# Tokens in a row for the state-space input product, and distant queries and keys stored by remainder

## The chip, the cores and the metric

The kernel runs on one core of one Trainium2 chip. The metric is device microseconds of one execution. A profiled execution of the kernel before gives the trace; its clock of TensorE (PE) was granted at 0.987 of full speed as a mean over the span.

## The reference, cut to what matters

Two blocks run one after the other on 1024 tokens of width 1024. The first has a gated MLP branch, a state-space (S5) branch and a mixture of experts; the second has dilated attention and a recurrent branch. All weights and activations are f32. Two places matter here.

```python
h = rms_norm(x, norm1_g[l])
p = h @ w_in[l]
uv = jax.nn.gelu(p[..., :o_s5], approximate=False)
s_in = p[..., o_s5:o_gate]          # 256 columns, the state-space input
...
DILATION_GROUPS = ((128, 1), (512, 4), (2048, 16))
...
# query t attends to t, t-r, t-2r, ..., t-window
t = t.astype(jnp.float32).reshape(B, L, dilation, H, Dh).transpose(0, 2, 1, 3, 4)
...
s = jnp.einsum('brnqhd,brnkhd->brnhqk', qs, kb) * (Dh ** -0.5)
```

There are three attention groups of four heads with 128 columns each. With 1024 tokens the second group works on four remainders of 256 tokens, and the kernel handles the third by eight remainders of 128 tokens and a mask for every other one.

## The kernel before, in words

**Big products.** Every f32 factor of a big product is split into a high and a low part (`K.split`: ScalarE copies the high part, L219; VectorE subtracts, L220), and `K.mm3` issues three matmuls per product, all recorded at L225. Attention's small products and the transposes (L228) use f32 directly; one such product is two matmul instructions, one transpose is one. Instructions of an engine run in the order in which they were laid out at compile time; a list scheduler of the framework lays them out by readiness, so an order can differ from the text of the program.

**State-space input.** `block1` loads the transposed x in eight pieces of 128 channels (`raw`, split into `xh`, `xl` by L1106 and L1107) and makes the product with the 256 state-space columns of `w_in` first. Its stationary operand takes every eighth token: `sl = slice(j, T, 8)`, so that for each of eight j the 128 rows of the result are tokens j, j+8, and so on. Eight pieces times eight j times three are 192 matmuls of 256 columns into four PSUM banks `ps_s`. ScalarE then copies them to `ss` with the token's norm as scale (L1166). The norms come from x read a second time by rows (`xj`, L1146, in tiles `m0` to `m3` twice over), squared on ScalarE (L1147), a reciprocal root on VectorE (`rsqrt`), and for the other layouts a diagonal `rd` (L1151), a product with ones on PE (L225, `ps<-m,sm`), `r_bc` (L1156) and `r_t` (L1158, L1159). `project(512, 0, ...)`, the first half of v, follows on PE with 192 matmuls of the same shape, whose stationary operands are 128 tokens in a row; its results fill the four other PSUM banks and wait there for `r_t` (gelu, L1174). The second half of v is next. `ss` is first read by the transposes of the first quarter of `s5` (L228, `ps<-sm,s`).

**Attention.** In `block2` the class `Pair` makes two output pieces of 128 columns by 1024 tokens with Strassen's seven half products, and hands halves to an output class by `one` (a ScalarE copy from PSUM, L389) or `two` (a VectorE sum of SBUF and PSUM, L394). `Spill` puts each 128x512 half into `st` (two buffers) and stores it in DRAM by SyncE (L390, L395). The first of a pair gets one `one` and one `two`, the second two `two`. The first twelve pairs of q, k and v hold group 0 beside group 1 of the same head (`near`); six pairs hold group 2. Beside later pairs, `Head` loads q, k and v of a head (L667, L671, L672) and works tile by tile: `scores` (L691 to L701), `turn` (transposes), `values`. In `scores` queries and keys are picked by `tok(g, m)`, 128 tokens in steps of 1, 4 or 8. A tile of width 256 has two products a block, one for the previous block of keys and one for the current one. `turn_v` transposes the values, picked by the same steps. `tick` advances this work by one step after each half product of a pair, so PE alternates between 12 matmuls of a pair and a step of attention.

```python
sl = slice(j, T, 8)
...
k.mm(pv[:, x, :128], s.q[:, tok(g, m)], s.kt[:, tok(g, m - back[g])], True, True)
k.mm(pv[:, x, W - 128:], s.q[:, tok(g, m)], s.kt[:, tok(g, m)], True, True)
```

Of the kernel before, what the change touches and what calls it, by code (L numbers as in the profile page):

```python
# [8 lines left out]
F32 = mybir.dt.float32  # L9
# [3 lines left out]
AF = mybir.ActivationFunctionType  # L13
# [7 lines left out]
T = 1024  # L21
# [133 lines left out]
class K:  # L155
    def __init__(s, tc, ins, ctx):
        s.tc, s.nc, s.i, s.ctx = tc, tc.nc, ins, ctx
        s.pp = ctx.enter_context(tc.tile_pool(name="pp", bufs=8, space=PSUM))
        s.dp = ctx.enter_context(tc.tile_pool(name="dp", bufs=1, space=DRAM))
        s.base = ctx.enter_context(tc.tile_pool(name="base", bufs=1))  # L160
        s.pool = s.base
        s.n = 0
        s.spare = {}
        s.last = {}
        s.turn = False
        s.wait = None
# [131 lines left out]
def bc(ap, axis, n):  # L298

    return ap.unsqueeze(axis).to_broadcast(list(ap.shape[:axis]) + [n] + list(ap.shape[axis:]))  # L300
# [57 lines left out]
def block2(k, out, dbg=None):  # L358
    nc, i, c = k.nc, k.i, k.c
    V, S, SY, GP = nc.vector, nc.scalar, nc.sync, nc.gpsimd  # L360
    dbg = dbg or {}
    ident = c("ident")
    MUL, ADD, SUB = OP.mult, OP.add, OP.subtract
    halves = [slice(0, 512), slice(512, 1024)]
# [4 lines left out]
    sq = k.t([128, SQW], "sq", pool=k.base)  # L369
# [11 lines left out]


    class Spill:
        def __init__(s, dst):
            s.dst = dst

        def one(s, h, p):
            st = k.t([128, 512], "st", 2)
            S.activation(st, p, AF.Copy)  # L389
            SY.dma_start(s.dst[:, halves[h]], st)  # L390

        def two(s, h, a, b):
            st = k.t([128, 512], "st", 2)
            V.tensor_tensor(st, a, b, op=ADD)  # L394
            SY.dma_start(s.dst[:, halves[h]], st)  # L395

    class Keep:
        def __init__(s, dst):
# [32 lines left out]
    qkv = {(n, g, j): dram(f"{n}d{g}{j}") for n in "qkv" for g in range(3) for j in range(4)}  # L431
    col = dict(q=Q0, k=K0, v=V0)
# [11 lines left out]

    w = lambda c: i["w_in2"][c // 128, 0]
    two = lambda c0, mk, x: tuple((w(c0 + y * 128), lambda y=y: mk(y)) for y in (x, x + 1))
    at = lambda n, g, j: (w(col[n] + g * 512 + j * 128), lambda: Spill(qkv[n, g, j]))
    near = [(at(n, 0, j), at(n, 1, j)) for j in range(4) for n in "qkv"]
    cols = []
    for f in range(0, 8, 2):  # L450
        cols += near[f:f + 2] + [two(U0, ukeep, f), two(GL0, lambda x: Spill(sgd[x]), f)]
    cols += near[8:]
    cols += [(at(n, 2, j), at(n, 2, j + 1)) for n in "qkv" for j in (0, 2)]
    cols += [two(GA0, lambda x: Spill(gad[x]), x) for x in (0, 2)]
    cols += [two(MG0, lambda x: Spill(mgd[x]), x) for x in (8, 10, 12, 14, 0, 2, 4, 6)]
    NI = len(cols)

# [198 lines left out]
    back = [1, 4, None]  # L656
    od = {(g, j): dram(f"od{g}{j}", (T, 130)) for g in range(3) for j in range(4)}
    otd = [dram(f"otd{j}") for j in range(4)]
    tok = lambda g, m: slice(toks[g][m][0], toks[g][m][0] + 127 * toks[g][m][1] + 1, toks[g][m][1])

    class Head:
# [20 lines left out]
        def scores(s, u):  # L682
            ms, W = tiles[s.g][u]
            g, n = s.g, len(ms)
            if u == 0:
                s.ss = k.t([128, 8, 2], "ss", 2)
            p = k.ps("pb")
            pv = p[:, :n * W].rearrange("p (m w) -> p m w", m=n)
            for x, m in enumerate(ms):
                if W == 256:  # L690
                    k.mm(pv[:, x, :128], s.q[:, tok(g, m)], s.kt[:, tok(g, m - back[g])], True, True)  # L691
                k.mm(pv[:, x, W - 128:], s.q[:, tok(g, m)], s.kt[:, tok(g, m)], True, True)
            s.sb = k.m(4)
            sv = s.sb[:, :n * W].rearrange("p (m w) -> p m w", m=n)
            mask = sq[:, SQ["mprev"][0]:SQ["mprev"][0] + 256] if W == 256 else cq("mtwo" if g == 2 else "mcur")
            V.tensor_tensor(sv, pv, bc(mask, 1, n), op=ADD)
            nm = s.ss[:, ms[0]:ms[0] + n, 1:2]
            V.tensor_reduce(nm, sv, axis=AX.X, op=OP.max, negate=True)
            V.tensor_scalar(nm, nm, SCALE, None, op0=MUL)
            for x, m in enumerate(ms):  # L700
                S.activation(sv[:, x, :], sv[:, x, :], AF.Exp, scale=SCALE, bias=s.ss[:, m, 1:2], accum_out=s.ss[:, m, 0:1])  # L701
# [121 lines left out]
    y, yh, yl, oh = (k.g("S", 12, dt) for dt in (F32, FR, FR, FR))  # L823
# [18 lines left out]
    def split(n, kk, src):  # L842
        h, l = part(n, kk)
        S.activation(h, src, AF.Copy)
        return V.tensor_tensor(l, src, h, op=SUB)  # L845
# [8 lines left out]
    def squares(half, t4, v):  # L854
        z = (a2 if half else F)[t4][:, :1024]
        return z, S.activation(z, xs[4 * half + t4], AF.Square, accum_out=v[:, t4:t4 + 1])
# [22 lines left out]
    for t4 in range(4):  # L879
        for h, hs in enumerate(halves):  # L880
            p = k.ps()
# [3 lines left out]
        z, sqd = squares(0, t4, va)  # L885
# [12 lines left out]
    for kk in range(8):  # L898
        dst = (a11 + a12)[kk]
# [35 lines left out]
    for kk in range(4):  # L935
        x = split("s4", kk, a12[kk])
# [102 lines left out]
    for m in range(8):  # L1039
        ga, y = k.m(m % 4), k.m(4 + m % 2)  # L1040
# [16 lines left out]
    for tt in range(8):  # L1057
# [4 lines left out]
        q = k.t([128, 2], "oq", 2)  # L1062
        fs, fb = [], k.g("gb")
        for h, hs in enumerate(halves):
            p = k.ps(("pa", "pb")[h])
# [9 lines left out]
        r = k.rsqrt(v, 1, "or")  # L1075
# [7 lines left out]
def block1(k, dbg=None):  # L1083
    nc, i = k.nc, k.i
    V, S, PE, SY, GP = nc.vector, nc.scalar, nc.tensor, nc.sync, nc.gpsimd
# [3 lines left out]
    c = lambda n: sm[:, SM[n][0]:SM[n][0] + SM[n][1]]  # L1089
# [9 lines left out]
    w_in, xT = i["w_in"], i["xT"]  # L1099
    ws_p, xh, xl = [], [], []  # L1100
    for kk in range(8):
# [3 lines left out]
        h, l = k.a(), k.a()  # L1105
# [7 lines left out]
    pv = [k.split(k.wload(w_in[2, q])) for q in range(2)]  # L1113


    ps_s = [k.ps("pb") for _ in range(4)]
    for kk in range(8):
        wh, wl = ws_p[kk // 4]
        for j in range(8):
            o = ps_s[j // 2][:, (j % 2) * 256:(j % 2) * 256 + 256]  # L1120
            sl = slice(j, T, 8)
            cs = slice((kk % 4) * 256, (kk % 4) * 256 + 256)
            k.mm3(o, xh[kk][:, sl], xl[kk][:, sl], wh[:, cs], wl[:, cs], kk == 0 and j % 2 == 0, kk == 7)

    vs = [k.g("U", 4, pool=k.pb) for _ in range(4)]

    def project(c0, hc, pc=None, pair=False):

        pc = pc or [k.split(k.wload(w_in[c0 // 256 + hc, q])) for q in range(2)]
        for tt in range(8):  # L1130
            if not pair or tt % 2 == 0:
                p = k.ps()
            o = p[:, tt % 2 * 256:tt % 2 * 256 + 256] if pair else p[:, :256]
            for kk in range(8):
                wh, wl = pc[kk // 4]
                cs = slice((kk % 4) * 256, (kk % 4) * 256 + 256)
                sl = slice(tt * 128, tt * 128 + 128)
                k.mm3(o, xh[kk][:, sl], xl[kk][:, sl], wh[:, cs], wl[:, cs], kk == 0, kk == 7)
            yield o, tt, vs[tt // 2][:, (tt % 2) * 512 + hc * 256:(tt % 2) * 512 + hc * 256 + 256]
# [13 lines left out]
    for h in range(2):  # L1153
        p = k.ps("pb")
# [4 lines left out]
    V.tensor_reduce(r_t, rd.rearrange("p (n t) -> p n t", n=8), axis=AX.X, op=OP.add)  # L1159


    ss = [k.g("s", 2) for _ in range(2)]
    for j in range(8):
        for hf in range(2):
            p = ps_s[j // 2][:, (j % 2) * 256 + hf * 128:(j % 2) * 256 + hf * 128 + 128].rearrange("p (g h) -> p g h", h=16)
            S.activation(ss[hf].rearrange("p (g j h) -> p g j h", g=8, j=8)[:, :, j, :], p, AF.Copy, scale=r_p[:, j:j + 1])  # L1166
    v0 = list(project(512, 0, pv, True))
    pv = [k.split(k.wload(w_in[3, q])) for q in range(2)]
    if "s" in dbg:
        for hf in range(2):  # L1170
            SY.dma_start(dbg["s"][:, hf * 1024:(hf + 1) * 1024], ss[hf])
# [55 lines left out]
    for q, n in enumerate(("lng", "lnb")):  # L1227
        a = i[n]
# [38 lines left out]
    for hf in range(2):  # L1267
        h, l = k.split(yT[hf], k.m(2 * hf, 1024, FR), k.m(2 * hf + 1, 1024, FR))
# [8 lines left out]
    for m in range(2):  # L1277
        sg = k.m(4 + m)
        for nh in range(2):
            p = k.ps()  # L1280
# [8 lines left out]
        h, l = k.split(sg, *((k.g("bb", 2, FR), k.g("bb", 2, FR)) if m == 0 else (k.g("r_bc", 1, FR, k.pb), k.g("yT", 2, FR, k.pb))))  # L1289
# [3 lines left out]
    for m in range(4):  # L1293
        h, l = k.g("ab", 8, FR), k.g("ab", 8, FR)
        for nh in range(2):
            p = k.ps("pb")
# [11 lines left out]
    for m in range(8):  # L1308
# [21 lines left out]
        for q in range(4):  # L1330
            h, l = (z.rearrange("p (m j c) -> p m j c", m=4, j=2)[:, m % 4] for z in mt[q][m // 4])
# [10 lines left out]
    for j in range(8):  # L1342
        xj = k.wload(xpv[:, j, :])
        for h in range(2):
            p = k.ps()
            hs = slice(h * 512, h * 512 + 512)
            for kk in range(8):
                sl = slice((kk % 4) * 256 + (j % 2) * 128, (kk % 4) * 256 + (j % 2) * 128 + 128)
# [596 lines left out]
def program(tc, ins, out):  # L1945
    with ExitStack() as ctx:
        k = K(tc, ins, ctx)
        block1(k)
        moe(k)
        block2(k, out)  # L1950
# [16 lines left out]
```

## Time and profile before

| what | us |
|---|---|
| runs: median of 3 (lowest to highest) | 2911.59 (2910.22 to 2913.25) |
| profiled execution, its own time | 2912.2 |
| span of its trace | 2910.4 |
| PE busy | 2804.7 |
| VectorE (DVE) busy | 2223.8 |
| ScalarE (ACT) busy | 1616.9 |

The span runs from the first to the last instruction; 1.8 us of the execution lie around it. In the trace PE is the matmul, PEld the load of the stationary operand that goes ahead of it, SPq the queue of SyncE that issues the DMAs. A tensor name such as `ps<-wh,A` is output, then the moving and the stationary operand. Matmuls overlap in the pipeline: the length of one is about 0.28 us or more, while the distance of their starts is what a stream costs.

### The profile page before, as it was taken

The numbers are of one execution on the slowest core, as the hardware profiler recorded it, in microseconds if no ns is written. First come the engines' busy times: TensorE is split into PE (matmuls) and PEld (weight loads), VectorE is DVE, ScalarE is ACT, GpSimd is POOL, SyncE is SP. The second block draws the span as 40 slices with busy tenths as digits, with TensorE's granted clock in tenths as the row PEclk, the third lists the DMA queues.
The fourth block names the chain that finished last, engine by engine and source line by source line (L and its number), as shares of the span: only waits on it lengthen the run. The fifth ranks groups of instructions, "written<-read, shape, count | busy, mean of one in ns | idle before, by whom it ended". The sixth has DMA issues, their size and how long they took to land. (4 is left out here: it accounts for less than half of the span.)

```text
span 2910.4 us, 37326 instructions
## 1 busy us (share of the span) xinstructions
PE 2804.7 (96%) x13441; PEld 2298.5 (79%) x13441; DVE 2223.8 (76%) x3619; ACT 1616.9 (56%) x2201; POOL 138.6 (5%) x106
## 2 busy tenths in 40 slices
PE   8999999949999999999999997999999999999998
PEld 8889887738888877777777775788888888888777
DVE  5967468589999888888888888878888554558774
ACT  4334334228888777777777776556665344444441
POOL 0000000020000000000000002100001100000000
PEclk9999999979999999999999999999999999999999
DMA  6123465558999999999999995223334644456762
GB/s 210 59 70 99 133 199 175 195 195 313 380 377 377 352 363 364 361 363 364 364 363 365 363 367 185 68 103 120 110 120 170 215 139 148 149 193 239 255 225 80
DMA packets 165993, 676.09 MB, mean 232 GB/s; under 512 B 18480, under 2 KB 28848, under 8 KB 125104
## 3 DMA queue, kind: packets, MB, share of 16 engines
q1 hardware_dynamic: 160912, 654.70, 61.5%
q0 software_dynamic: 4896, 19.01, 2.5%
q8 instruction: 105, 1.72, 0.2%
q14 instruction: 80, 0.66, 0.1%
HBM read 586.97 MB, written 84.57 MB: 231 GB/s over the span
## 5 line engine op out<-in xcount | busy, mean ns | idle before, releaser
L225 PE MATMUL ps<-A,wh 128*128 128x512 f32 x1920 | 603.5, 395 | 4.7 <-DVE A L845 1.9
L225 PEld LDWEIGHTS ps<-A,wh 128*128 128x128 f32 x1920 | 357.6, 188 | 81.1 <-DVE A L845 2.3
L225 PE MATMUL ps<-A,wl 128*128 128x512 f32 x960 | 375.6, 391 | 0.0
L1825 DVE TENSOR_TENSOR wl<-A,wh 128x1024 fp32r<-128x1024 f32 x253 | 308.8, 1221 | 38.7 <-ACT wh L1821 37.0
L1825 DVE TENSOR_TENSOR ml<-A,mh 128x1024 fp32r<-128x1024 f32 x253 | 308.5, 1219 | 9.2 <-ACT mh L1821 2.6
L225 PE MATMUL ps<-S,wh 128*128 128x512 f32 x960 | 306.1, 400 | 7.0 <-DVE u L530 4.8
L219 ACT ACTIVATE wh<-wr 128x512 fp32r<-128x512 f32 (+2 forms) x168 | 154.7, 922 | 242.9 <-PE ps L225 189.2
L1821 ACT ACTIVATE wh<-A 128x1024 fp32r<-128x1024 f32 x256 | 270.3, 1056 | 23.8 <-PE ps L225 23.8
L1821 ACT ACTIVATE mh<-A 128x1024 fp32r<-128x1024 f32 x256 | 270.2, 1055 | 20.9 <-PE ps L225 20.9
L220 DVE TENSOR_TENSOR wl<-wr,wh 128x1024 fp32r<-128x1024 f32 (+2 forms) x166 | 175.6, 1058 | 66.5 <-ACT wh L219 51.8
L225 PE MATMUL ps<-wl,xh 128*128 128x512 f32 x520 | 209.1, 402 | 10.1 <-DVE wl L1825 10.1
L225 PEld LDWEIGHTS ps<-S,wh 128*128 128x128 f32 x960 | 180.4, 191 | 47.4 <-DVE u L530 6.6
L225 PEld LDWEIGHTS ps<-A,wl 128*128 128x128 f32 x960 | 180.2, 188 | 39.5 <-issue 0.7
L225 PE MATMUL ps<-wh,xl 128*128 128x512 f32 x520 | 205.4, 395 | 0.0
L225 PE MATMUL ps<-ml,xh 128*128 128x512 f32 x520 | 204.1, 392 | 0.5 <-DVE ml L1825 0.5
L225 PE MATMUL ps<-mh,xl 128*128 128x512 f32 x520 | 203.2, 391 | 0.0
L225 PE MATMUL ps<-S,wl 128*128 128x512 f32 x480 | 190.5, 397 | 0.0
L225 PE MATMUL ps<-wh,xh 128*128 128x512 f32 x520 | 188.2, 397 | 0.0
L225 PE MATMUL ps<-mh,xh 128*128 128x512 f32 x520 | 186.7, 393 | 0.2 <-ACT mh L1821 0.2
L225 PE MATMUL ps<-wh,A 128*128 128x256 f32 (+1 forms) x704 | 159.5, 319 | 8.1 <-ACT wh L219 8.1
L225 PEld LDWEIGHTS ps<-wh,A 128*128 128x128 f32 x704 | 128.8, 218 | 12.4 <-ACT wh L219 8.1
L228 PE MATMUL ps<-sm,m 128*128 128x128 f32 (+1 forms) x692 | 102.2, 278 | 28.5 <-DVE m L1460 14.2
(508 smaller groups left out, 5534.2 us busy)
## 6 DMA issues: line engine op xcount, KB each, us to landing
A<-in_w_up_dram SPq DMA_DIRECT2D x125, 1024.0 KB, 8.0
A<-in_w_down_dram SPq DMA_DIRECT2D x65, 1024.0 KB, 7.1
A<-in_w_gate_dram SPq DMA_DIRECT2D x64, 1024.0 KB, 6.4
wr<-in_w_gate_dram SPq DMA_DIRECT2D x124, 512.0 KB, 7.1
mr<-in_w_down_dram SPq DMA_DIRECT2D x59, 1024.0 KB, 7.0
wr<-in_w_in_dram SPq DMA_DIRECT2D x82, 512.0 KB, 4.0
wr<-in_w_mod_dram SPq DMA_DIRECT2D x24, 512.0 KB, 4.4
wr<-in_w_ing_dram SPq DMA_DIRECT2D x16, 512.0 KB, 4.5
```

The costliest lines, as they stand in the source:

```text
L219: s.parts = (s.nc.scalar.activation(hi, raw, AF.Copy), (eng or s.nc.vector).tensor_tensor(lo, raw, hi, op=OP.subtract))
L220: (eng or s.nc.vector).tensor_tensor(lo, raw, hi, op=OP.subtract))
L225: s._pe(out, s.nc.tensor.matmul(out, a, b, start=start, stop=stop, skip_group_check=True))
L228: s._pe(out, s.nc.tensor.transpose(out, a, ident))
L1821: a = S.activation(h, raw, AF.Copy)
L1825: (GP if n < 6 else V).tensor_tensor(l, raw, h, op=OP.subtract)
```

## The change

The state-space product takes 128 tokens in a row as stationary operand. Its four banks are copied to SBUF (in the first half of each of the tiles `vs`, which are written for good only later), stored to a new DRAM tensor `sd` with one row per token, and read back with eight consecutive tokens per partition into `m0` and `m1`. The copies to `ss` then read these. The first half of v and the next weights stand ahead of the copies in the text.

`Spill` gets a step: 4 for queries and keys of group 1, 8 for those of group 2. The copy or sum reads both its inputs by remainder and writes `st` in runs of one remainder. For step 8 the store puts eight runs of 64 tokens (256 bytes) per partition into the rows of 128 tokens per remainder. `scores` then takes 128 neighbouring columns, and a tile of width 256 makes one product of 256 keys a block, in two runs of 128. Values stay in token order.

```diff
-        def __init__(s, dst):
-            s.dst = dst
+        def __init__(s, dst, step=1):
+            s.dst, s.step = dst, step
+
+        def of(s, *z):
+            st = k.t([128, 512], "st", 2)
+            if s.step == 1:
+                return st, (st,) + z
+            by = lambda y: y.rearrange("p (i r) -> p r i", r=s.step)
+            return st, (st.rearrange("p (r i) -> p r i", r=s.step),) + tuple(map(by, z))
 
         def one(s, h, p):
-            st = k.t([128, 512], "st", 2)
-            S.activation(st, p, AF.Copy)
-            SY.dma_start(s.dst[:, halves[h]], st)
+            st, (o, p) = s.of(p)
+            S.activation(o, p, AF.Copy)
+            s.put(h, st)
 
         def two(s, h, a, b):
-            st = k.t([128, 512], "st", 2)
-            V.tensor_tensor(st, a, b, op=ADD)
-            SY.dma_start(s.dst[:, halves[h]], st)
+            st, (o, a, b) = s.of(a, b)
+            V.tensor_tensor(o, a, b, op=ADD)
+            s.put(h, st)
+
+        def put(s, h, st):
+            if s.step == 8:
+
+                d = s.dst.rearrange("p (r h i) -> p h r i", r=8, h=2)
+                SY.dma_start(d[:, h], st.rearrange("p (r i) -> p r i", r=8))
+            else:
+                SY.dma_start(s.dst[:, halves[h]], st)
...
-    at = lambda n, g, j: (w(col[n] + g * 512 + j * 128), lambda: Spill(qkv[n, g, j]))
+    at = lambda n, g, j: (w(col[n] + g * 512 + j * 128), lambda: Spill(qkv[n, g, j], (1, 4, 8)[g] if n in "qk" else 1))
...
+                own = lambda z: z[:, m * 128:(m + 1) * 128]
+                keys = own(s.kt)
                 if W == 256:
-                    k.mm(pv[:, x, :128], s.q[:, tok(g, m)], s.kt[:, tok(g, m - back[g])], True, True)
-                k.mm(pv[:, x, W - 128:], s.q[:, tok(g, m)], s.kt[:, tok(g, m)], True, True)
+                    keys = s.kt.rearrange("p (m c) -> p m c", c=128)[:, m - back[g]:m + 1:back[g]]
+                k.mm(pv[:, x], own(s.q), keys, True, True)
...
-            sl = slice(j, T, 8)
+            sl = slice(j * 128, j * 128 + 128)
...
     vs = [k.g("U", 4, pool=k.pb) for _ in range(4)]
+    sd = k.dp.tile([T, 256], F32, name="sd", tag="sd")
+    for q, p in enumerate(ps_s):
+        z = vs[q][:, :512]
+        S.activation(z, p, AF.Copy)
+        SY.dma_start(sd[q * 256:(q + 1) * 256].rearrange("(n t) d -> t n d", t=128), z.rearrange("t (n d) -> t n d", n=2))
...
+    sq = [k.m(q) for q in range(2)]
+    for q in range(2):
+        SY.dma_start(sq[q], sd.rearrange("(c j) d -> c (j d)", j=8)[:, q * 1024:(q + 1) * 1024])
+    v0 = list(project(512, 0, pv, True))
+    pv = [k.split(k.wload(w_in[3, q])) for q in range(2)]
+
     ss = [k.g("s", 2) for _ in range(2)]
     for j in range(8):
         for hf in range(2):
-            p = ps_s[j // 2][:, (j % 2) * 256 + hf * 128:(j % 2) * 256 + hf * 128 + 128].rearrange("p (g h) -> p g h", h=16)
+            p = sq[j // 4][:, (j % 4) * 256 + hf * 128:(j % 4) * 256 + hf * 128 + 128].rearrange("p (g h) -> p g h", h=16)
             S.activation(ss[hf].rearrange("p (g j h) -> p g j h", g=8, j=8)[:, :, j, :], p, AF.Copy, scale=r_p[:, j:j + 1])
-    v0 = list(project(512, 0, pv, True))
-    pv = [k.split(k.wload(w_in[3, q])) for q in range(2)]
```

## Rows read from the trace of the kernel before

**Rows 1.** The page, part 1: busy time and share of each engine.

```profile
PE 2804.7 (96%) x13441; PEld 2298.5 (79%) x13441; DVE 2223.8 (76%) x3619; ACT 1616.9 (56%) x2201; POOL 138.6 (5%) x106
```

**Rows 2.** Busy time by stretch (first line: the columns).

```profile
core 0: us, PE busy (x) PEld busy (x) DVE busy (x) ACT busy (x) POOL busy (x), PEclk, DMA share, GB/s
12.00:54.90 42.90, 42.90 (x181) 42.90 (x180) 21.04 (x104) 18.62 (x26) 2.12 (x2) 1.00 0.76 266
55.20:66.40 11.20, 11.20 (x96) 11.20 (x95) 4.42 (x17) 3.75 (x11) 0.49 (x1) 1.00 0.22 70
...
1860.00:2280.00 420.00, 413.60 (x1777) 336.27 (x1778) 330.35 (x420) 222.46 (x259) 24.74 (x23) 0.99 0.39 134
2280.00:2600.00 320.00, 318.82 (x1695) 277.87 (x1694) 165.95 (x275) 142.50 (x361) 0.00 (x0) 1.00 0.46 153
```

**Rows 3.** PE in order of time: start, length, line, [idle before <-releaser].

```profile
54.87 0.52 PE L225 MATMUL ps<-wh,A 128*128 128x256 f32 x2
...
66.49 1.88 PE L225 MATMUL ps<-m,sm 128*128 128x512 f32 x4
```

**Rows 4.** VectorE in order of time, block1.

```profile
23.91 1.28 DVE L1107 SCALAR_TENSOR_TENSOR A<-wr,sm,A 128x1024 fp32r<-128x1024 f32 x1 [0.59 <-ACT A L1106]
...
59.53 1.22 DVE L1151 TENSOR_TENSOR m<-sm,rqy 128x1024 f32<-128x1024 f32 x1
...
70.30 1.22 DVE L1159 TENSOR_REDUCE r_t<-m 128x8 f32<-128x1024 f32 x1
```

**Rows 5.** ScalarE in order of time, block1.

```profile
32.27 1.06 ACT L219 ACTIVATE wh<-wr 128x1024 fp32r<-128x1024 f32 x1 [5.93 <-PE ps L225]
33.23 1.04 ACT L1147 ACTIVATE m<-m 128x1024 f32<-128x1024 f32 x1
...
43.43 1.06 ACT L1147 ACTIVATE m<-m 128x1024 f32<-128x1024 f32 x1
...
55.31 1.06 ACT L219 ACTIVATE wh<-wr 128x1024 fp32r<-128x1024 f32 x1 [10.73 <-PE ps L225]
59.45 2.69 ACT L1166 ACTIVATE s<-ps,rqy 128x128 f32<-128x128 f32 x10 [3.08 <-DVE rqy L272]
```

**Rows 6.** SyncE's queue: x read by rows (L1146), its issues and their landing.

```profile
22.53 15.31 SPq L1146 DMA_DIRECT2D m<-in_xp_dram  x8
...
DMA to landing us min/median/max: 3.6/5.6/9.0
```

**Rows 7.** PE in order of time: the first reader of `ss`.

```profile
107.65 0.66 PE L228 MATMUL ps<-sm,s 128*128 128x128 f32 x4
```

**Rows 8.** PE in order of time: score products (L225) and a transpose of values (L228).

```profile
2301.42 1.06 PE L225 MATMUL ps<-m,m 128*128 128x128 f32 x8
2309.12 0.61 PE L225 MATMUL ps<-m,m 128*128 128x128 f32 x4
2316.22 2.12 PE L225 MATMUL ps<-m,m 128*128 128x128 f32 x8
...
2321.39 1.12 PE L228 MATMUL ps<-sm,m 128*128 128x128 f32 x8
...
2545.58 2.18 PE L225 MATMUL ps<-m,m 128*128 128x128 f32 x8
```

**Rows 9.** PE in order of time: f32 products of 256 columns in `s5`.

```profile
140.07 1.03 PE L225 MATMUL ps<-m,s5E 128*128 128x256 f32 x4
...
141.38 0.60 PE L225 MATMUL ps<-m,s5E 128*128 128x256 f32 x2
```

**Rows 10.** Groups by line and shape: xcount, busy us, mean ns, idle before.

```profile
L394 DVE TENSOR_TENSOR st<-u,ps 128x512 f32<-128x512 f32 x96 | 65.4, 681 | 61.3 <-PE ps L225 59.7 <-DMA vd<-st 1.3
...
L220 DVE TENSOR_TENSOR A<-m,A 128x256 fp32r<-128x256 f32 x32 | 19.8, 669 | 0.4
...
L1179 DVE TENSOR_TENSOR U<-U,gt 128x256 f32<-128x256 f32 x16 | 6.6, 419 | 9.8 <-ACT gt L1178 9.8
```

**Rows 11.** DMA issues with median landing time (2250 to 2700 us), and one pair's stores.

```profile
qd<-st SPq DMA_DIRECT2D x8, 256.0 KB, 2.3
...
2298.25 8.43 SPq L395 DMA_DIRECT2D qd<-st  x3
```

## The prediction

> **What bounds the kernel now.** I read the page first: PE is busy for 2804.7 us of the span, the next engine for 2223.8 [rows 1]. A share is a mean, so I took both stretches that the change touches. While the state-space input runs (12 to 54.9 us) and while attention runs beside the projections (2280 to 2600 us) PE has next to no gap, 42.9 of 42.9 and 318.8 of 320, at a full clock, with VectorE at about half [rows 2]. So a microsecond less of PE's stream should be a microsecond less of the whole, unless a wait appears that PE's own slowness hid. Then I compared paces of matmuls that differ in nothing but the step between their stationary columns; that is where the gain must come from. Last came the chains that PE's slowness hides: the norms [rows 3 to 6] and the way of the halves out of PSUM [rows 10, 11].
>
> **State-space product.** Before, 181 matmuls start in 42.9 us, 0.237 us each; right behind them the first half of v, with the same shape, moving weights and x tiles but 128 tokens in a row, starts 96 in 11.2 us, 0.117 each [rows 2]. The pace changes where the operand changes, at 55 us [rows 3]. 192 x 0.120 = **23.1 us** less. Can x come fast enough? The last low part of x is ready at 25.2 us [rows 4]; a piece then needs 24 x 0.117 = 2.8 us, eight 22.4, so PE, starting near 8 and held a little by the first weights, ends at about 32 and not at 55. Bound below: if x held it all the same, the end is still no later than 25.2 + 2.8 plus the pieces behind it, so little is lost.
>
> **What is late next.** PE's queue holds, 11.3 us behind the end of the product, the product of ones with `rd` (66.49 us) [rows 3]; everything behind it on PE waits for it. `rd` needs all eight squares. Before, the first square started at 33.23 because ScalarE stood 5.93 us before it, waiting for PE to free a weight buffer [rows 5]; that wait goes, as the fourth piece ends near 21. x by rows is issued from 22.53 and lands after 5.6 us [rows 6], so I put the first square at 29 and the last, as before 10.2 us behind it [rows 5], to end near 40. From the end of the last square (44.5) to the end of `rd` (60.75) went 16.3 us [rows 4, 5], of which some 10 are the weight split behind ScalarE's 10.73 us wait for PE's end of product [rows 5]; 6 remain. So `rd` is ready near 46. PE arrives at 32 + 11.3 = 43.4 if the ones keep their place, and near 38 if they move up, since their bank now comes free by four early copies and not by the copies to `ss`. The stall is 2 to 8 us: I take **5**, the middle, and keep 0 and 8. `r_t` came 5.0 us behind the ones [rows 3, 4], so near 52, while the first half of v then ends near 61: no second stall.
>
> **The way through DRAM.** Added: four copies of 128x512 on ScalarE (a copy of 1024 columns takes 1.06 us [rows 5]; half of that and a fixed part, so about 0.6 each), four stores, two loads. It ends near 50 and `ss` some 6 us later; the first reader on PE stood at 107.65 [rows 7], so near 90 after the change. The cover is 30 us; without it the whole trip, about 15 us, would be paid. The stores go on SyncE's queue, and what waits behind a waiting store there is the loads of x by rows: that is a rival. The 16 copies to `ss` stay; they read SBUF. Cost: 0.
>
> **Scores.** Eight instructions take 1.06 us with steps of 1, 2.12 with steps of 4 (group 1) and 2.18 with steps of 8 (group 2) [rows 8]. Group 1 has three such tiles per head, group 2 two, four heads each: 12 x 1.06 + 8 x 1.12 = **21.7 us** less. The products of 256 keys give nothing more: an f32 instruction of 256 columns costs (1.03 - 0.60) / 2 = 0.215 us [rows 9], two of 128 columns 2 x (1.06 - 0.61) / 4 = 0.225 [rows 8], so 88 pairs give 0.9 at most. I take 22 for both. Nothing waits longer for scores: the turn that follows stands behind the same 12 matmuls as before.
>
> **The halves on their way out.** The steps do not vanish, they move to VectorE and ScalarE. 28 sums (8 pairs of group 1 with two, 4 of group 2 with three) and 4 copies now read by remainder. No row has a strided operand in PSUM. The nearest is the split of 128x256 with one operand in steps of 8: 0.669 us against 0.419 for a plain sum of that size [rows 10], 0.25 more per 256 columns, so 0.50 more on 0.681 for a sum. Below, nothing; above, both operands pay, 1.0. I take 0.5, since that row is the same engine and step: 14 us of VectorE. VectorE stands idle 61.3 us ahead of 96 such sums, nearly all waiting for PE [rows 10], and PE lost only 6.4 of 420 us in the busiest part, VectorE at 79% [rows 2]. I charge **1.5 us**, with 0 and 6 as ends.
>
> [...]
>
> **DMA.** 16 stores of group 2 write runs of 256 bytes in place of 2 KB. They land in 2.3 us now; three stores of a pair take 8.43 us, about 4 apart, and the two buffers leave roughly 7 us before a third sum needs the first again [rows 11]. So up to threefold landing costs nothing, and attention reads group 2 last. Cost: 0.
>
> **Sum.** 23.1 - 5 + 22 - 1.5 = 38.6 us less. The profiled execution took 2912.2 us (span 2910.4 and 1.8 around it); that gives 2873.6, and the median of the runs shown is 0.6 below it: **2873 us**.
>
> **Rivals.**
> *No stall* (0.24): the ones stand later on PE or the squares end sooner. For it: x lands as early as 3.6 us [rows 6]. Against it: the bank comes free earlier. 5 us better: 2868.
> *The queue* (0.14): the stores of `sd` stand on SyncE ahead of x by rows, as in the text. Then x starts near 36, when the copies are done, in place of 22.53; the last square, 22 us behind the first issue before with 4.6 of them the weight buffer's wait [rows 5, 6], ends near 53, `rd` near 59, and PE stalls 17 us, not 5: 2885. Against it: before, what was ready first was queued first.
> *The step is not the cause* (0.04): the values' transposes take their stationary operand in steps of 4 and need only 1.12 us for eight [rows 8]. If the state-space product is slow by something else, 18 us go: 2891. Against it: the same tiles at half the cost right behind it.
> *The stores* (0.04): if runs of 256 bytes land after 10 us, 12 sums wait 2.6 us each, up to 31: 2904. [...]
> *Slower: the sums hold PE* (0.04). A sum frees PE's bank, and the splits of the next pair queue behind it. Its cover is 61.3 / 96 = 0.64 us [rows 10]. To eat 40 us, 28 sums must each exceed this by 1.45, so from about 2.8 us a sum the kernel is slower; at 3.2 it ends near 2924. Against it: that is eight times the extra that the split's row shows.
>
> **Numbers.** My forecast has 0.50. Faster by over 0.2% (5.8 us, about what a measurement of this kernel can tell from no change) are all but the last rival and a sliver between: 0.95, same 0.01, slower 0.04. The range takes in the forecast with its ends (stall 0 to 8, sums 0 to 6), *no stall* and *the queue*: 2862 to 2889.
>
> **What would show it.** PE at about 0.117 us per matmul from 8 us, the first half of v starting near 32, a wait of PE for `rd` near 43, copies to `ss` done before 60, PE's first reader of `ss` some 18 us earlier. In attention 1.06 for every full score tile. `st` sums near 1.2 us and no new wait of PE for them. Wrong if the product keeps 0.24, if SyncE's stores precede x by rows, or if PE waits for `st` or `u` by tens of microseconds.

## The result and the profile after

Four runs of the changed kernel have a median of 2874.03 us (2868.33 to 2875.23); four of the kernel before, on the same chip, 2911.38 (2910.22 to 2913.25). The ratio, estimated from all of these runs, is 0.9868, 95% interval 0.9853 to 0.9882: faster, by 37 us, 1 us from the forecast. The profiled execution took 2875.23 us, its span 2873.5, the mean granted clock 0.987 in both kernels.

First the page, part 1, of the changed kernel, beside [rows 1].

```profile
PE 2763.0 (96%) x13353; PEld 2253.5 (78%) x13353; DVE 2232.4 (78%) x3619; ACT 1618.4 (56%) x2205; POOL 138.4 (5%) x106
```

PE is busy 41.7 us less and the span is 36.9 us shorter; VectorE gained 8.6 us of work, so it stands idle 45.5 us less. The bound is the same. Then the stretches [rows 2]: the start, the state-space product, and the two of attention, which come some 18 us earlier now.

```profile
core 0: us, PE busy (x) PEld busy (x) DVE busy (x) ACT busy (x) POOL busy (x), PEclk, DMA share, GB/s
8.70:14.70 6.00, 5.96 (x26) 5.67 (x27) 6.00 (x19) 3.74 (x4) 0.00 (x0) 1.00 0.78 251
15.00:33.00 18.00, 18.00 (x153) 18.00 (x152) 15.47 (x81) 11.84 (x15) 0.00 (x0) 1.00 0.91 315
1842.00:2262.00 420.00, 413.66 (x1790) 336.03 (x1789) 339.49 (x424) 224.00 (x260) 24.58 (x23) 1.00 0.39 134
2262.00:2560.00 298.00, 296.06 (x1604) 252.05 (x1603) 168.09 (x275) 141.11 (x361) 0.00 (x0) 1.00 0.53 167
```

The first two stretches in the kernel before:

```profile
8.70:14.70 6.00, 5.67 (x25) 5.37 (x23) 6.00 (x19) 3.45 (x4) 0.00 (x0) 1.00 0.77 244
15.00:33.00 18.00, 18.00 (x77) 18.00 (x76) 11.82 (x56) 8.07 (x9) 0.00 (x0) 1.00 0.85 297
```

From 15 to 33 us PE starts 153 matmuls in 18 us, 0.118 each; the kernel before started 77 there. But the stretch ahead of it holds only 26 in 6 us, where the kernel before had 25. PE in order of time [rows 3] shows both paces, and the product of ones:

```profile
10.98 0.41 PE L225 MATMUL ps<-wh,A 128*128 128x256 f32 x1
11.19 0.41 PE L225 MATMUL ps<-wl,A 128*128 128x256 f32 x1
...
14.82 0.46 PE L225 MATMUL ps<-wh,A 128*128 128x256 f32 x2
15.12 0.28 PE L225 MATMUL ps<-wl,A 128*128 128x256 f32 x1
...
49.88 1.96 PE L225 MATMUL ps<-m,sm 128*128 128x512 f32 x4 [1.38 <-ACT s L1196]
```

Until 14.8 us starts lie 0.213 us apart, from there 0.12. PE had run next to nothing before: from 2 to 8.7 us it is busy for 0.01. The PEclk column says 1.00 in both stretches, so the granted clock does not show the difference; the starts do. In the kernel before they lay 0.24 apart in both, so that it could not be seen. The product ends near 34.4 us (55.1 before).

SyncE's queue, in order of time, answers to [rows 6]:

```profile
21.89 10.28 SPq L1170 DMA_DIRECT2D m<-in_xp_dram  x6
33.62 2.98 SPq L1149 DMA_DIRECT2D sd<-U  x4
36.65 1.98 SPq L1170 DMA_DIRECT2D m<-in_xp_dram  x2
40.86 0.80 SPq L1188 DMA_DIRECT2D m<-sd  x2
```

and the seventh square on ScalarE to [rows 5]:

```profile
42.18 1.06 ACT L1171 ACTIVATE m<-m 128x1024 f32<-128x1024 f32 x1 [4.01 <-DMA m<-in_xp_dram]
```

Two of the eight loads of x by rows stand behind the stores of `sd`; the seventh square waits 4.01 us for them, and the last ends at 44.6. On VectorE, `rd` (now L1175) is then ready at 49.8 [rows 4]:

```profile
48.55 1.22 DVE L1175 TENSOR_TENSOR m<-sm,rqy 128x1024 f32<-128x1024 f32 x1
```

The ones start right behind it, at 49.88. Their 1.38 us wait is put down to ScalarE's L1196, which is not what they read: its copy from 48.55 had ended by 48.95, and the tensor `m` with `rd` in it is VectorE's.

In attention, the score products by shape [rows 8, 10], and the sums and copies on their way out:

```profile
L225 PE MATMUL ps<-m,m 128*128 128x256 f32 x88 | 23.0, 380 | 0.0
L225 PE MATMUL ps<-m,m 128*128 128x128 f32 x104 | 14.5, 278 | 1.9 <-DMA m<-kd 1.9
L402 DVE TENSOR_TENSOR st<-u,ps 128x512 f32<-128x512 f32 x96 | 76.9, 801 | 53.5 <-PE ps L225 50.7 <-DMA vd<-st 1.6 <-DMA qd<-st 0.9
L397 ACT ACTIVATE st<-ps 128x512 f32<-128x512 f32 x32 | 18.5, 579 | 0.0
```

The same groups of the kernel before, where they were not shown:

```profile
L225 PE MATMUL ps<-m,m 128*128 128x128 f32 x280 | 59.8, 362 | 1.2 <-PE ps L228 0.8 <-DMA m<-kd 0.4
...
L389 ACT ACTIVATE st<-ps 128x512 f32<-128x512 f32 x32 | 18.6, 580 | 0.0
```

Scores fell from 59.8 to 23.0 + 14.5 = 37.5 us of PE. Sums rose by 11.5 us, 0.41 for each of the 28; the copies cost the same with four of them by remainder, 579 ns in the mean and 580 before. VectorE's time line has the 28 one by one, first step 4, then step 8:

```profile
2214.84 1.06 DVE L402 TENSOR_TENSOR st<-u,ps 128x512 f32<-128x512 f32 x1
2218.62 1.04 DVE L402 TENSOR_TENSOR st<-u,ps 128x512 f32<-128x512 f32 x1
...
2258.20 1.19 DVE L402 TENSOR_TENSOR st<-u,ps 128x512 f32<-128x512 f32 x1 [0.17 <-PE ps L225]
2261.43 1.15 DVE L402 TENSOR_TENSOR st<-u,ps 128x512 f32<-128x512 f32 x1 [0.91 <-DMA qd<-st]
```

The short stores land after a median of 3.3 us (2.3 before [rows 11]):

```profile
qd<-st SPq DMA_DIRECT2D x8, 256.0 KB, 3.3
```

**Where the time went**, by landmarks that both kernels have. The first multiplication of the branches' results by their gate (L1325 before, L1353 after) and the first add of the output product to x (L1351, L1379) stand on VectorE's time line, before:

```profile
424.43 0.68 DVE L1325 TENSOR_TENSOR m<-ps,m 128x512 f32<-128x512 f32 x1
499.59 1.29 DVE L1351 TENSOR_TENSOR wr<-ps,wr 128x512 f32<-128x512 f32 x2 [3.10 <-DMA wr<-in_xp_dram]
```

and after:

```profile
405.71 0.68 DVE L1353 TENSOR_TENSOR m<-ps,m 128x512 f32<-128x512 f32 x1
482.35 1.29 DVE L1379 TENSOR_TENSOR wr<-ps,wr 128x512 f32<-128x512 f32 x2 [4.52 <-DMA wr<-in_xp_dram]
```

The first moved by 18.7 us, the second by 17.2; it waits for x by rows, 4.52 us where it was 3.10, and by 508 us the shift is 16.0. In the second block the first copies into `st`, group by group with the first and last start, stood at 1850.0 before

```profile
L389 ACT ACTIVATE st<-ps x32: 576/580/589, 1850.0 to 2677.7; 128x512 f32<-128x512 f32 x32
```

and stand at 1834.0 after:

```profile
L397 ACT ACTIVATE st<-ps x32: 572/579/590, 1834.0 to 2638.0; 128x512 f32<-128x512 f32 x32
```

There the shift is still 16.0. It is 17.4 in the middle of the second block's projections (2152.00 and 2134.56), before any score product, and 36.9 at the end. So in these two traces the state-space part left 16.0 us, and the second block, attention's, gave 20.9. Why 1.4 of these come ahead of the scores was not traced.

### The profile page after: what moved, and what is told of

Its sections match the earlier page's. It is cut to its first block, busy times and chain, and to the rows that moved or that the text cites. A ratio compares the mean times of both kernels' runs of the same rounds, so it can differ in the third digit from the quotient of the medians.

```text
span 2873.5 us, 37166 instructions
## 1 busy us (share of the span) xinstructions
PE 2763.0 (96%) x13353; PEld 2253.5 (78%) x13353; DVE 2232.4 (78%) x3619; ACT 1618.4 (56%) x2205; POOL 138.4 (5%) x106
## 5 line engine op out<-in xcount | busy, mean ns | idle before, releaser
L225 PE MATMUL ps<-A,wh 128*128 128x512 f32 x1920 | 603.6, 395 | 4.5 <-DVE u L541 1.9
L225 PEld LDWEIGHTS ps<-A,wh 128*128 128x128 f32 x1920 | 357.1, 188 | 81.9 <-issue 2.6
L225 PE MATMUL ps<-A,wl 128*128 128x512 f32 x960 | 375.9, 392 | 0.0
L1853 DVE TENSOR_TENSOR wl<-A,wh 128x1024 fp32r<-128x1024 f32 x253 | 308.8, 1221 | 38.5 <-ACT wh L1849 36.9
L225 PE MATMUL ps<-S,wh 128*128 128x512 f32 x960 | 304.4, 398 | 5.5 <-DVE u L546 3.4
L225 PE MATMUL ps<-wl,xh 128*128 128x512 f32 x520 | 209.1, 402 | 10.1 <-DVE wl L1853 10.1
L220 DVE TENSOR_TENSOR wl<-wr,wh 128x1024 fp32r<-128x1024 f32 (+2 forms) x166 | 175.4, 1056 | 53.1 <-ACT wh L219 38.4
L225 PEld LDWEIGHTS ps<-S,wh 128*128 128x128 f32 x960 | 178.9, 189 | 45.7 <-DVE u L546 5.1
L225 PEld LDWEIGHTS ps<-A,wl 128*128 128x128 f32 x960 | 180.2, 188 | 39.6 <-issue 0.7
L225 PE MATMUL ps<-wh,xl 128*128 128x512 f32 x520 | 205.3, 395 | 0.0
L225 PE MATMUL ps<-ml,xh 128*128 128x512 f32 x520 | 204.1, 393 | 0.5 <-DVE ml L1853 0.5
L225 PE MATMUL ps<-mh,xl 128*128 128x512 f32 x520 | 203.3, 391 | 0.0
L225 PE MATMUL ps<-S,wl 128*128 128x512 f32 x480 | 189.1, 394 | 0.0
L225 PE MATMUL ps<-wh,xh 128*128 128x512 f32 x520 | 188.2, 397 | 0.0
L225 PE MATMUL ps<-mh,xh 128*128 128x512 f32 x520 | 186.6, 393 | 0.2 <-ACT mh L1849 0.2
L225 PE MATMUL ps<-wh,A 128*128 128x256 f32 (+1 forms) x704 | 143.5, 299 | 8.7 <-ACT wh L219 8.7
L228 PE MATMUL ps<-sm,m 128*128 128x128 f32 (+1 forms) x692 | 102.4, 278 | 28.6 <-DVE m L1488 14.2
L225 PEld LDWEIGHTS ps<-wl,xh 128*128 128x128 f32 x520 | 97.9, 188 | 39.9 <-DVE wl L1853 18.5
```

The source lines that it names most:

```text
L220: (eng or s.nc.vector).tensor_tensor(lo, raw, hi, op=OP.subtract))
L225: s._pe(out, s.nc.tensor.matmul(out, a, b, start=start, stop=stop, skip_group_check=True))
L228: s._pe(out, s.nc.tensor.transpose(out, a, ident))
L1853: (GP if n < 6 else V).tensor_tensor(l, raw, h, op=OP.subtract)
```

## The experiments

**Each half alone.** Run `e1_a_only` keeps the state-space part, `e2_b_only` attention's.

```diff
# e1_a_only: after, but
+    ... lambda: Spill(qkv[n, g, j])
+                    k.mm(pv[:, x, :128], s.q[:, tok(g, m)], s.kt[:, tok(g, m - back[g])], True, True)
+                k.mm(pv[:, x, W - 128:], s.q[:, tok(g, m)], s.kt[:, tok(g, m)], True, True)
# e2_b_only: after, but
+            sl = slice(j, T, 8)
...
```

Expected of the first:

> Only the state-space product has tokens in a row; queries and keys are stored and read as before. Theory (two separate gains): 17 to 18 us faster than before, near 2894, PE's score tiles at 2.12 and 2.18 us. Rival (attention's part carries it, the product is bound by x or gives its gain back in the round trip): within 6 us of before.

Of the second:

> Only queries and keys of groups 1 and 2 are written by remainder; the state-space product keeps its steps of eight tokens. Theory: 19 to 21 us faster than before, near 2891, score tiles at 1.06 us, the state-space product at 0.24 us per matmul. Rival (the sums and short stores give the gain back): less than 10 us faster.

Measured, beside 2914.47 for the kernel before on that chip: 2895.62 (ratio 0.9929, 0.9913 to 0.9946) and 2893.75 (0.9925, 0.9909 to 0.9942). Medians fall by 18.9 and 20.7 us, 39.6 together where the whole change gives 37.4; the product of the ratios, 0.9855, lies in the interval of the whole change. The two halves are about equal and add up within the noise.

**Which step of the state-space product costs.** One run each, with the stationary columns in steps of 2 and of 4 (the stores of `sd` put the rows back in order).

```diff
# e7_step2
-            sl = slice(j * 128, j * 128 + 128)
+            sl = slice(256 * (j // 2) + j % 2, 256 * (j // 2) + j % 2 + 255, 2)
# e8_step4
-            sl = slice(j * 128, j * 128 + 128)
+            sl = slice(512 * (j // 4) + j % 4, 512 * (j // 4) + j % 4 + 509, 4)
```

> State-space product with stationary operands of every second token; the store to DRAM puts the rows back. [...] Rival (any step costs): 0.24 us.

> The same with every fourth token. [...] Rival (the price grows with the step, or four is still free): between 0.12 and 0.20 us.

The stretch from 15 to 33 us, with step 2:

```profile
15.00:33.00 18.00, 18.00 (x152) 18.00 (x151) 15.62 (x83) 12.39 (x16) 0.00 (x0) 1.00 0.94 322
```

and with step 4:

```profile
15.00:33.00 18.00, 18.00 (x78) 18.00 (x79) 12.03 (x59) 8.93 (x10) 0.00 (x0) 1.00 0.82 297
```

A step of 2 is free (152 matmuls start, 153 with tokens in a row), a step of 4 costs all that 8 costs (78 and 77). The times agree: 2867.94 and 2893.33 us, the latter within 1 us of attention's half alone. Apart from the rows that the stores of `sd` write, behind the product, nothing else differs between the two, so the step is the cause. Why the price sets in between 2 and 4 was not shown.

**Which operand of the scores costs.** Queries are the stationary operand, keys the moving one. In `e3_q_only` only queries are stored by remainder, and keys are still picked in steps; in `e4_k_only` the other way round. Both make two products of 128 keys.

```diff
# e3_q_only (e4_k_only: "k" for "q", steps on s.q)
+    ... Spill(qkv[n, g, j], (1, 4, 8)[g] if n in "q" else 1)
+                    k.mm(pv[:, x, :128], own(s.q), s.kt[:, tok(g, m - back[g])], True, True)
+                k.mm(pv[:, x, W - 128:], own(s.q), s.kt[:, tok(g, m)], True, True)
```

> As the changed kernel, but only the queries (stationary operand) are by remainder; the keys (moving operand) keep their steps, with two products of 128 keys. Theory (the stationary operand's step costs): score tiles of groups 1 and 2 at about 1.06 us, total within 4 us of the changed kernel. Rival (the moving operand's step costs): 2.1 us, about 20 us slower than the changed kernel.

> The mirror: only the keys (moving operand) are by remainder, the queries (stationary operand) keep their steps. Theory (the stationary operand's step costs): score tiles of groups 1 and 2 at about 2.1 us, about 20 us slower than the changed kernel. Rival (the moving operand's step costs): 1.06 us.

A tile of group 1 with steps on the keys alone:

```profile
2297.86 1.97 PE L225 MATMUL ps<-m,m 128*128 128x128 f32 x8
```

and on the queries alone:

```profile
2298.76 2.03 PE L225 MATMUL ps<-m,m 128*128 128x128 f32 x8
```

Either alone doubles the tile (1.06 without), and both together make 2.12 [rows 8]. All score products take 56.7 us with queries in runs, 57.6 with keys in runs, 59.8 with neither. One run each gave 2889.84 and 2893.05 us, little below the 2895.62 without either. Both expectations, and both rivals in them, took one operand for the cause, and both missed. Neither is the cause by itself: each hides behind the other, and half of this part of the change would have been worth little.

**Are 256 keys a product worth anything?** In `e9_two_products` both are in runs, but a block again takes two products of 128.

```diff
-                k.mm(pv[:, x], own(s.q), keys, True, True)
+                    k.mm(pv[:, x, :128], qq, kk_(m - back[g]), True, True)
+                k.mm(pv[:, x, W - 128:], qq, kk_(m), True, True)
```

(`qq` and `kk_(y)` are 128 neighbouring columns of queries and keys.)

> The changed kernel, but tiles of width 256 make two products of 128 keys each in place of one of 256. Theory (an f32 product streams by columns): 0 to 1 us slower than the changed kernel. Rival (an instruction's fixed part counts): 3 us or more slower.

```profile
L225 PE MATMUL ps<-m,m 128*128 128x128 f32 x280 | 38.2, 277 | 1.6 <-DMA m<-kd 1.5
```

38.2 us against 37.5, and 2873.83 us (0.9861, 0.9844 to 0.9877): 0.7 us of PE, not to be told from nothing in the time.

**What the way out costs.** `e5_spill_only` stores by remainder, but leaves `scores` as it was, so that scores mix tokens and the output is not the reference's: the cost of the sums and short stores without their gain.

> The changed kernel's sums, copies and stores by remainder stay, but scores pick queries and keys by steps as before, so the scores of groups 1 and 2 mix tokens (the output is not the reference's). Against the kernel with the state-space part alone this is the bare price of the way out. Theory (hidden): within 3 us of that kernel, near 2895. Rival (sums or short stores hold PE): 8 us or more slower than that kernel.

2896.34 us beside 2913.68 (0.9941, 0.9924 to 0.9957), 17.3 us less, where the state-space part alone gave 18.9. The difference, 1.6 us by medians and 0.0012 by ratios (3.5 us), lies inside the intervals: it is small, and its size is not settled. VectorE's sums show why:

```profile
L402 DVE TENSOR_TENSOR st<-u,ps 128x512 f32<-128x512 f32 x96 | 76.9, 801 | 58.7 <-PE ps L225 57.0 <-DMA vd<-st 1.4
```

The full 11.5 us more is there, and VectorE still waits 57.0 us for PE (59.7 before [rows 10]): it had room.

**From where on do sums hold PE?** `e6_sums_three_times` does each of the 28 sums by remainder three times.

```diff
-            V.tensor_tensor(o, a, b, op=ADD)
+            for _ in range(1 if s.step == 1 else 3):
+                V.tensor_tensor(o, a, b, op=ADD)
```

> Each of the 28 sums by remainder is issued three times (same values), so each costs VectorE 3.3 us or more, past the 2.8 us from which the prediction's slower rival says the kernel is slower than before. Theory (VectorE has room beside PE): VectorE busy 61 us more, total 2 to 25 us above the changed kernel. Rival (every microsecond past the cover holds PE): 50 us or more above the changed kernel, slower than before.

2893.36 us beside 2913.68 (0.9935, 0.9918 to 0.9951), 20.3 us less than before. The sums:

```profile
L403 DVE TENSOR_TENSOR st<-u,ps 128x512 f32<-128x512 f32 x152 | 137.9, 913 | 38.7 <-PE ps L225 35.1 <-DMA vd<-st 2.7
```

and PE's waits from 1820 to 2600 us, with the us in total, the count and the longest:

```profile
PE ps L225 <- DVE st L403: 6.6, 5, 2.1
```

137.9 - 76.9 = 61 us more of VectorE cost 17 us by medians (20.3 us are left of 37.4). In this run alone PE waits for `st`, but for 6.6 us only; where the other 10 us go was not traced. One sum by remainder now takes (137.9 - 68 x 0.681) / 28 = 3.3 us; at 3.2 my slower rival had the kernel at 2924.

**PE at work before x arrives.** `e10_warm` lays 20 bf16 products of zeros ahead of the loads of x; nothing reads them.

```diff
+    zw = k.m(5)[:, :512].bitcast(BF)
+    nc.gpsimd.memset(zw, 0.0)
+    pw = k.ps()
+    for _ in range(20):
+        k.mm(pw, zw[:, :128], zw[:, :512], True, True)
```

> The changed kernel with 20 bf16 matmuls of zeros on PE ahead of the first real ones, while x is still being loaded; nothing reads them. [...] Rival (x or its low parts pace the first matmuls): pace unchanged, total the same or higher.

PE in order of time:

```profile
1.75 7.45 PE L225 MATMUL ps<-m 128*128 128x512 bf16 x20 [1.75 <-POOL m L1120]
8.84 0.83 PE L225 MATMUL ps<-wh,A 128*128 128x256 f32 x4
...
10.98 0.28 PE L225 MATMUL ps<-wh,A 128*128 128x256 f32 x1
11.10 0.28 PE L225 MATMUL ps<-wl,A 128*128 128x256 f32 x1
```

and its first stretch:

```profile
8.70:14.70 6.00, 5.85 (x47) 5.51 (x45) 6.00 (x19) 3.15 (x4) 0.00 (x0) 1.00 0.77 242
```

At 11 us the pace is 0.12 and no longer 0.213; 47 matmuls start where 26 did. So the slow start is gone where PE is at work ahead of it, and x does not hold the first matmuls. The median is 2869.18 us (2866.44 to 2869.97; ratio 0.984, 0.9823 to 0.9856), against 2873.83 (2873.39 to 2875.8) for two products on the same chip: 4.65 us, of which merging can hold no more than its 0.7, and more than the 28 x 0.093 = 2.6 that the pace of the first 28 accounts for. How the pace comes to 4.65 is not shown. The ones start at 49.95 (last section), no earlier than the 49.88 of the changed kernel, since they wait 2.93 us there and not 1.38. PE's first reader of `ss` starts at 87.96, 0.9 us ahead of the changed kernel's 88.90, and 3.2 ahead of the 91.17 with two products, where the granted clock fell to 0.57 and the ones took 3.47 us in place of 1.95 (last section). And the intervals of all three ratios touch or overlap, with one execution of the changed kernel at 2868.33: that the zeros make it faster is likely, not settled.

**The queue.** `e11_act_queue` issues the stores of `sd` on ScalarE's queue, so that x by rows is not behind them; `e12_warm_act_queue` adds the zeros.

```diff
-        SY.dma_start(sd[q * 256:(q + 1) * 256].rearrange("(n t) d -> t n d", t=128), z.rearrange("t (n d) -> t n d", n=2))
+        S.dma_start(sd[q * 256:(q + 1) * 256].rearrange("(n t) d -> t n d", t=128), z.rearrange("t (n d) -> t n d", n=2))
```

> The changed kernel with the four stores of the state-space input issued by ScalarE's queue, so that the last two loads of x by rows don't stand behind them on SyncE's. Theory: the last square ends near 40 us and not 44.6, the product of ones loses its wait of 1.4 us, total 1 to 2 us lower. Rival (the order on PE, not the norms, sets it): no change beyond 1 us.

> Both of the last two edits together. Theory (independent): 2 to 5 us below the changed kernel. Rival: what one gains is taken up by the wait for the norms, no more than the better one alone.

The order changed as meant, in SyncE's queue of `e11_act_queue`:

```profile
22.53 13.29 SPq L1170 DMA_DIRECT2D m<-in_xp_dram  x8
...
47.76 0.81 SPq L1188 DMA_DIRECT2D m<-sd  x2
```

and PE in order of time shows that nothing was won:

```profile
49.72 1.95 PE L225 MATMUL ps<-m,sm 128*128 128x512 f32 x4 [1.58 <-issue]
62.18 0.38 PE L225 MATMUL ps<-wh,A 128*128 128x256 f32 x1 [0.19 <-ACT wh L219]
65.33 0.38 PE L225 MATMUL ps<-wl,A 128*128 128x256 f32 x1 [2.77 <-DVE wl L220]
```

All eight loads are issued in one go, the last square ends at 43.3 us instead of 44.6, and the ones still start at 49.7: what they wait for then is VectorE, where a weight's split of 1.23 us (L220, from 44.82) now comes ahead of `rd`, ready at 49.6. The reads of `sd` slid from 40.86 to 47.76, and a wait of 2.77 us for a weight's low part is new. 2879.79 us (0.9874, 0.9858 to 0.9891), no better than with SyncE's queue, and by medians 6 us behind two products on the same chip; with the zeros 2870.21 (0.9851, 0.9835 to 0.9867), no better than the zeros alone. The first expectation missed; the second has its number, 3.8 us below the changed kernel, but by the zeros alone, as its rival said.

## Why the prediction was right, point by point

The mechanism held: PE's stream sets the time (41.7 us less of it, 36.9 less of the span), the steps of its operands set its pace (153 matmuls in 18 us and not 77), and what the change adds elsewhere is nearly hidden. That the total came within 1 us is luck in part. The state-space part was to leave 18.1 us and left 16.0 in the traces, after misses of 2 to 4 us either way; attention was to give 20.5 and gave 20.9.

- **State-space product, 23.1 us: 20.7.** The mechanism held (`e7_step2`, `e8_step4`). What failed is the pace that I took for all 192 matmuls: the row it came from lay at 55 us, where PE had been at work for long. The first 28 or so start 0.213 us apart, 28 x 0.093 = 2.6 us more, and in `e10_warm`, where PE works before them, they start 0.12 apart. That x would not hold it came true.
- **Stall at the ones, 5 us: 1.4,** below the 2 to 8 I gave, and near the rival *no stall*. Two errors against each other. The last square came at 44.6, not 40, because two loads did stand behind the stores of `sd`, the *queue* rival's order in part; `rd` was ready at 49.8, not 46. But PE had 14.1 us of other matmuls between the product's end and the ones, not 11.3 or fewer, so it got there at 48.5. The step that failed is "the ones keep their place or move up": they moved down. Of 20.7 - 1.4 = 19.3 us, 18.7 were there at 405.71 and 16.0 at the start of the second block (18 forecast). The add's longer wait for x by rows, 4.52 us for 3.10, is 1.4 of what was given back in between; the rest I did not trace.
- **The way through DRAM, 0: held.** `ss` was copied by 55 us, its first reader on PE came at 88.90 (107.65 before, [rows 7]), and that is by PE's own order: 33 us of cover.
- **Scores, 22 us: 22.3.** Every tile now takes 1.03 to 1.06 us, the merged ones too, and merging gave 0.7 of the 0.9 allowed.
- **Sums, 0.50 us each and 1.5 in all:** 0.41 each in the mean (0.36 to 0.41 with steps of 4, 0.41 to 0.51 with steps of 8), and 1.6 by medians in `e5_spill_only`, where the intervals cannot tell it from nothing. The value from the split's row was nearer than the upper end, 1.0, at which both operands pay. Of ScalarE's 32 copies, four of which now read PSUM in steps of 8 and write runs, none takes more than 590 ns (589 before).
- **Short stores, 0: held.** Stores in runs of 256 bytes land after 3.3 us, 1 us later than in runs of 2 KB (2.3) and far inside threefold, and VectorE waited for them once, 0.9 us.
- **The rivals.** *Not the step* and *the stores* fell. *The queue* came true in its order and not in its price: it put the stall at 17 us as if all eight loads moved behind the stores, where only two did. *Slower* fell by more than I gave: at 3.2 us a sum the kernel is still 20 us faster. Its cover was taken as a mean, 0.64 us a sum; but 61 us of extra VectorE work cost 17. My reading, which no run isolates, is that a late sum holds nothing until the bank or buffer that it frees is next wanted.
- **The range.** Its lower end, 2862, is not worked out: the best ends of its terms, a stall of 0 and sums of 0, give 2866.5.

## What to carry to other kernels

Where two matmul streams of one shape differ in pace, compare the steps of their operands before anything else, both of them, since the cost of one hid that of the other here (1.97 and 2.03 us a tile with one in steps, 2.12 with both, 1.06 with neither); in the state-space product steps of 2 f32 were free (152 matmuls in 18 us, 153 in runs), and steps of 4 and 8 doubled the cost of it (78 and 77) and of the score products (2.12 and 2.18 us a tile). Paying for runs on the way out of PSUM was cheap here (11.5 us of VectorE, 1.6 of the time by medians), where VectorE waited 59.7 us for PE anyway. A price from a row late in the span need not hold for the first microseconds of an engine that stood idle (0.213 us a matmul here, not 0.12): look at the pace of the starts. Something for PE to do before its data came mended the pace; the next wait, 2.93 us in place of 1.38, took most of that up again.

## What the runs showed of the hardware

- **Steps don't add up.** 1.06 us a tile without, 1.97 and 2.03 with one operand in steps of 4, 2.12 with both. And a transpose with its stationary operand in steps of 4 takes 1.12 [rows 8].
- **ScalarE read PSUM in steps of 8 at no cost** (590 ns at most, 589 before), while VectorE's sum of SBUF and PSUM goes from 0.681 us to 1.04 to 1.09 with steps of 4 and 1.09 to 1.19 with steps of 8. Which of its two inputs VectorE pays for was not tried.
- **Behind a stall of PE the granted clock fell in some runs and not in others.** The ones waited 3 us in `e9_two_products` as in `e10_warm`. In the first, by stretch, the granted clock fell to 0.57 behind it:

```profile
50.00:52.00 2.00, 1.36 (x2) 0.83 (x3) 1.76 (x2) 1.83 (x5) 0.00 (x0) 0.57 0.99 379
52.00:54.00 2.00, 2.00 (x4) 0.73 (x3) 0.00 (x0) 0.89 (x2) 0.00 (x0) 0.58 1.05 395
```

and PE's ones, in order of time, took 3.47 us:

```profile
50.64 3.47 PE L225 MATMUL ps<-m,sm 128*128 128x512 f32 x4 [3.04 <-ACT s L1198]
```

In the second it stayed at 1.00, and they took 1.95:

```profile
49.95 1.95 PE L225 MATMUL ps<-m,sm 128*128 128x512 f32 x4 [2.93 <-ACT s L1201]
```

and the clock, by stretch:

```profile
50.00:52.00 2.00, 2.00 (x7) 1.04 (x8) 1.23 (x1) 2.00 (x7) 0.00 (x0) 1.00 1.02 383
```

In `e1_a_only` it fell too, to 0.50 from 50 to 52 us, behind a wait of 2.98 us, and in `e12_warm_act_queue` to 0.62 and then 0.52, behind one of 2.29; the ones took 3.34 and 3.32. Stalls of one length were thus followed by a full or by a lower clock, and what decides is open. Whether this is why executions of the changed kernel lie up to 7 us apart (2868.33 to 2875.23; the kernel before 3) was not tried.
